# TensorE's order through an attention stage: a fixed order with a list of projections for each head, in place of a scheduler's

## The chip, the cores and the metric

The kernel runs on one core of a Trainium2 chip. The metric is the device time of one execution in microseconds. A core has a matrix engine (TensorE, in the profile PE, with its weight loads as PEld), a vector engine (VectorE, DVE), an activation engine (ScalarE, ACT), a general engine (GpSimd, POOL) and an engine that issues most of the transfers (SyncE, SP). Each works through a queue of its own in order, and they meet at semaphores.

## The reference

One layer of a streaming encoder over 512 frames of width 1024, all in float32:

```python
xn = rmsnorm(x, norm_mix_g)
q, k, v, xr, gr, ga, gb = split(xn @ w_in)
ya = chunked_band_attention(q, k, v, rel_table) @ w_attn_out    # 16 heads of 64
yb = (rg_lru(causal_depthwise_conv(xr)) * gelu(gr)) @ w_rnn_out
g_a, g_b = sigmoid([ga, gb] + b_merge)
h = x + (g_a * ya + g_b * yb) @ w_o
g, up = split(rmsnorm(h, norm_ffn_g) @ w_ffn_in)
out = rmsnorm(h + (silu(g) * up) @ w_ffn_out, final_norm_g)
```

In the attention each frame reads its own chunk of 64 frames and the eight before it, with a learned bias by relative distance for each head. With 512 frames the band reaches back to the start, so it is causal by chunks.

## The kernel before

Every float32 operand of a projection is split into a high and a low part (`split`, L78: ScalarE copies the high part, L80, VectorE subtracts it, L81), and a product is three matmuls, high-high, high-low and low-high (`mm3`, L72, lines L74 to L76). Weights are loaded to `raw` tiles and split to `whl` tiles; `weights` (L243) also prefetches the next chunk. Four `whl` buffers hold two chunks of weights, so a half of a new chunk is split when a projection has done with the half that had its buffer.

The order of the work is: normalize x, the projections and the recurrence of branch B, q and k of the first pair of heads, v of the first four heads, the output projection of branch B (`po_yb0` to `po_yb7`), then the attention, then `po_ya` (the output projection of the attention), `po_h`, and the feed-forward part.

The attention handles 16 heads, two to a pair. A pair needs a q tile and a k tile (`q_tile` L593, `k_tile` L604), four heads need four v tiles (`v_tile` L627). A q or k tile is 24 matmuls 512 wide, a v tile 24 matmuls 256 wide. Each is emptied from its bank by ScalarE and VectorE (q: L600 and L601; k: L611, L612, L613, and GpSimd's copy L614). For each head:

- `scores(h)` (L638): four score tiles s0 to s3, one for each block of 128 queries, 256, 256, 384 and 512 wide, two matmuls each (L651, L652). VectorE adds the bias and finds the negated maximum (L654, and a read of the accumulator m), ScalarE takes the exponential with the sum (L655), VectorE inverts the sums of all four (L656), GpSimd scales the four tiles (L658). The bias is a transfer (L424) and a memset of GpSimd (L425), with two buffers.
- `transposed(h, prob)` (L661): ten transposes (L670) of the probabilities to three banks, pT_0, pT_1 and pT_2, which are split to `pp` tiles for the next step.
- `weigh(h, pp)` (L679): eight matmuls (L690) to a bank `o`, emptied by ScalarE and VectorE (L691, L692).

The banks of the accumulator memory are eight: four with the tag "mm" (`mm_tile`, L69), two with "s", two with "t". Before the change the score tiles 0, 1 and 3 take the two "s" banks in turn and tile 2 an "mm" bank; pT_0 and pT_1 take "t"; pT_2, o and all projections of the attention take "mm".

The loop over the heads calls `transposed(h)`, `scores(h + 1)`, `fill`, `weigh(h)`, `fill`. `fill` takes projections from one list in the order q1, k1, q2, k2, v of heads 4 to 7, q3, and so on, ending with the gates `gate(0, 4)` to `gate(0, 7)` (tiles `po_ga`), until the work spent reaches a due sum. The calls do not fix the engines' order: the kernel is built under a scheduler that follows a simulated timeline and places every engine's instructions, TensorE's among them, by priority and by when it thinks they are ready. It chooses the bank of each tile as well. So in the program before, score tiles and weighings stand between matmuls of a projection; `s_3`, for instance, stands inside the projection that follows it.

Of the kernel before, what the change touches and what calls it, by code (L numbers as in the profile page):

```python
# [8 lines left out]
F32 = mybir.dt.float32  # L9
# [5 lines left out]
P = 128  # L15
D = 1024
S = 512
KT = D // P
NT = S // P
HEADS = 16  # L20
# [16 lines left out]
def block_kernel(ctx: ExitStack, tc: tile.TileContext, x, norm_mix_g, w_in, b_merge, rel_table,  # L37
# [25 lines left out]
    ps = ctx.enter_context(tc.tile_pool(name="ps", bufs=2, space=PSUM))  # L63
    dr = ctx.enter_context(tc.tile_pool(name="dr", bufs=1, space=bass.MemoryType.DRAM))

    def f(ap):
        return ap.bitcast(F32)

    def mm_tile(name, tag="mm"):  # L69
        return ps.tile([P, S], F32, tag=tag, bufs=4 if tag == "mm" else 2, name=name)  # L70
# [172 lines left out]
    def weights(name, ahead=1):  # L243
        prefetch(index[name] + 1 + ahead)
        return made[index[name]]

    def project(o, whl, c, xs, lo=0, hi=S):

        n = len(xs)
        for k in range(n):  # L250
            at = slice(c * P, (c + 1) * P)
            mm3(o[:, lo:hi], whl(0, k, at), whl(1, k, at),
                xs[k][:, 0, lo:hi], xs[k][:, 1, lo:hi], k == 0, k == n - 1)
# [108 lines left out]
    def features(pl, tag, name):  # L362

        t = pl.tile([P, KT, 2, S], F32R, tag=tag, name=name)
        return t, [t[:, k] for k in range(KT)]
# [13 lines left out]
    _, xnT = features(xnp, "xn", "xnT")  # L379
# [165 lines left out]
    def tile_of(name, c, tag="mm", ahead=1):  # L545

        whl = weights(name, ahead)
        if (name, c) in first:
            po = first[name, c]
            project(po, whl, c, xnT, 256, S)  # L550
        else:
            po = mm_tile(f"po_{name}_{c}", tag)
            project(po, whl, c, xnT)
        return po
# [5 lines left out]
    def gate(w, j):  # L560
        po = tile_of(f"g{'ab'[w]}{j - j % 2}", j % 2)
        act.activation((ta, zB)[w][j], po[:], AF.Tanh, bias=hb[:, 16 + 8 * w + j:17 + 8 * w + j], scale=0.5)
# [30 lines left out]
    def q_tile(pr):  # L593
        po = mm_tile(f"po_q{pr}")
        project(po, weights(f"qk{pr}"), 0, xnT)
        q = qk_pool(pr).tile([P, 2, S], F32R, tag="qk", bufs=3, name=f"q{pr}")
        for e in range(2):
            own, other = halves(e)
            src = backwards(po[own, :])
            act.activation(blocks(q[own, e]), src, AF.Copy, scale=0.125)  # L600
            dve.scalar_tensor_tensor(blocks(q[other, e]), src, 0.125, blocks(f(q[own, e])), ALU.mult, ALU.subtract)  # L601
        qk[pr] = [q]

    def k_tile(pr):  # L604
        po = mm_tile(f"po_k{pr}")
        project(po, weights(f"qk{pr}"), 1, xnT)
        kh = qk_pool(pr).tile([P, 2, S], F32R, tag="qk", bufs=3, name=f"kh{pr}")
        kl = qk_pool(pr).tile([P, 2, S], F32R, tag="qk", bufs=3, name=f"kl{pr}")
        for e in range(2):
            own, other = halves(e)  # L610
            act.activation(kh[own, e], po[own, :], AF.Copy)  # L611
            dve.tensor_sub(kl[own, e], po[own, :], f(kh[own, e]))  # L612
            act.activation(kh[other, e], po[own, :], AF.Copy)  # L613
            pool.tensor_copy(kl[other, e], kl[own, e])  # L614
        qk[pr] += [kh, kl]
# [11 lines left out]
    def v_tile(gr, t):  # L627
        wv = weights(f"v{gr}")
        po = mm_tile(f"po_v{gr}_{t}", "mm" if gr else "t")
        for k in range(KT):  # L630
            mm3(po[:, 0:256], xnT[k][:, 0, t * P:(t + 1) * P], xnT[k][:, 1, t * P:(t + 1) * P],
                wv(0, k, whole), wv(1, k, whole), k == 0, k == KT - 1)
        v = aw.tile([P, 2, 4, HD], F32R, tag="v", bufs=8, name=f"v{gr}_{t}")
        split(v[:, :, 0::3], v[:, :, 1:3], po[:, 0:256].rearrange("p (a b d) -> p a b d", a=2, b=2))
        vs.setdefault(gr, []).append(v)


    def scores(h):  # L638
        pr, e = divmod(h, 2)
        q, kh, kl = qk[pr]  # L640
        bias = bias_tile(h)
        lsum = cp.tile([P, NT], F32, tag="lsum", bufs=2, name=f"l{h}")
        nmax = cp.tile([P, NT], F32, tag="nmax", bufs=2, name=f"m{h}")
        rl = cp.tile([P, NT], F32, tag="rl", bufs=2, name=f"rl{h}")
        prob = [aw2.tile([P, (qb + 1) * P], F32, tag=f"p{qb}", name=f"p{h}_{qb}") for qb in range(NT)]
        for qb in range(NT):
            w = (qb + 1) * P
            wm = max(w, 256)
            sc = mm_tile(f"s{h}_{qb}") if qb == 2 else ps.tile([P, S], F32, tag="s", bufs=2, name=f"s{h}_{qb}")
            qs = q[:, e, qb * P:(qb + 1) * P]  # L650
            pe.matmul(sc[:, 0:wm], qs, kh[:, e, 0:wm], start=True, stop=False)  # L651
            pe.matmul(sc[:, 0:wm], qs, kl[:, e, 0:wm], start=False, stop=True)  # L652

            dve.tensor_tensor_reduce(prob[qb][:], sc[:, 0:w], bias[:, S - w:S], -1.0, 3e38, ALU.add, ALU.min, nmax[:, qb:qb + 1])  # L654
            act.activation(prob[qb][:], prob[qb][:], AF.Exp, bias=nmax[:, qb:qb + 1], scale=-1.0, accum_out=lsum[:, qb:qb + 1])  # L655
        dve.reciprocal(rl[:], lsum[:])  # L656
        for qb in range(NT):
            pool.tensor_scalar(prob[qb][:], prob[qb][:], rl[:, qb:qb + 1], 1.0, ALU.mult, ALU.mult)  # L658
        return prob

    def transposed(h, prob):  # L661

        pp = [aw2.tile([P, 2, S], F32R, tag="pt", bufs=4, name=f"pp{h}_{i}") for i in range(3)]
        pool.memset(f(pp[2][:, :, 256:384]), 0.0)
        for i, kbs in enumerate(((0,), (1,), (2, 3))):
            pt = mm_tile(f"pT{h}_{i}") if i == 2 else ps.tile([P, S], F32, tag="t", bufs=2, name=f"pT{h}_{i}")
            for kb in kbs:
                for qb in range(kb, NT):
                    at = qb - min(kb, 2) if kb < 3 else 2
                    pe.transpose(pt[:, at * P:(at + 1) * P], prob[qb][:, kb * P:(kb + 1) * P], ident[:])  # L670
            for at, lo, n in (((0, 0, 512),), ((0, 0, 384),), ((0, 0, 256), (384, 256, 128)))[i]:
                split(pp[i][:, 0, at:at + n], pp[i][:, 1, at:at + n], pt[:, lo:lo + n])
        return pp
# [5 lines left out]
    def weigh(h, pp):  # L679
        pr, e = divmod(h, 2)  # L680
        own, other = halves(e)
        if e == 0:
            oacc.append(tg_.tile([P, S], F32, tag="tg", name=f"oacc{pr}"))
        acc = oacc[pr]
        po = mm_tile(f"o{h}")
        for kb in range(NT):
            i, lo, n = ((0, 0, 512), (1, 0, 384), (2, 0, 256), (2, 256, 256))[kb]
            st = vs[pr // 2][kb][:, pr % 2, 2 * e:2 * e + 2].rearrange("p a d -> p (a d)")
            for part in range(2):
                pe.matmul(po[:, S - n:S], st, pp[i][:, part, lo:lo + n], start=kb == 0 and part == 0, stop=kb == NT - 1 and part == 1)  # L690
        act.activation(acc[own, :], po[other, :], AF.Copy)  # L691
        dve.tensor_add(acc[own, :], po[own, :], acc[own, :])  # L692
        if e == 1:
            if pr % 2 == 0:
                aT_pairs.append(rnp.tile([P, 2, 2, S], F32R, tag="big", bufs=4, name=f"aT{pr}"))
            o = aT_pairs[-1][:, pr % 2]
            split(blocks(o[:, 0]), blocks(o[:, 1]), backwards(acc[:]))
            aT.append(o)


    steps = []
    for pr in range(1, HEADS // 2):
        steps.append((1.0, lambda pr=pr: q_tile(pr)))
        steps.append((1.0, lambda pr=pr: k_tile(pr)))
        if pr in (2, 4, 6):
            for t in range(NT):
                steps.append((0.5, lambda pr=pr, t=t: v_tile(pr // 2, t)))
    for j in range(4, KT):
        steps.append((1.0, lambda j=j: gate(0, j)))
    spent = 0.0  # L710

    def fill(upto):
        nonlocal spent
        while steps and spent < upto:
            w, what = steps.pop(0)
            what()
            spent += w

    for t in range(NT):
        v_tile(0, t)  # L720
# [1 line left out]
    for j in range(KT):  # L722
        if j == 6:
            prob = scores(0)
        po = mm_tile(f"po_yb{j}")
        project(po, weights(f"yb{j - j % 2}"), j % 2, rnn)
        dve.scalar_tensor_tensor(zB[j], zB[j], 1.0, po[:], ALU.add, ALU.mult)
    for h in range(HEADS):
        pp = transposed(h, prob)
        if h + 1 < HEADS:  # L730
            prob = scores(h + 1)
        fill(1.25 + 1.5 * h)
        weigh(h, pp)
        fill(2.0 + 1.5 * h)
    aw2_stack.close()
    wo_stack, wop = opened("wo", 4)
    extra["wo1"] = wop
# [3 lines left out]
    _, mT = features(xnp, "xn", "mT")  # L741
# [113 lines left out]
    sc_stack, sc = opened("sc", 2)  # L855
# [83 lines left out]
    ks = list(range(0, FT, 4))  # L939
# [51 lines left out]
```

## Time and profile before

| | |
|---|---|
| median of 3 runs | 888.18 us (887.58 to 888.22) |
| the profiled execution | 887.22 us |
| its span, first to last instruction | 885.4 us |
| TensorE's clock | 1.000 of full |
| TensorE busy, share of the span | 98% |
| the attention, from the first transposes to the last weighing | about 248 to 449 us of the span |

The span is the time between the first and the last instruction of the profiled execution; 1.8 us of its own time lie around it. A row of the timeline has the start from the span's start in us, the duration in us, the engine, the line of the code, the operation, what it writes and reads with the shapes, and how many instructions are merged in the row. In brackets stands how long the engine had been idle ahead of it, and which instruction ended that. A row of the windows has the stretch, its length, then the busy time of PE, PEld, DVE, ACT and POOL, TensorE's granted clock, and the transfers' share and rate. The steps from the start of one matmul to that of the next are shorter than the durations, since matmuls overlap.

### The profile page before, as it was taken

Reading aid. Unit: us, or ns where it says so; the run is one execution under the profiler, and the core shown is the slowest. Engines: PE = TensorE matmul, PEld = TensorE weight load, DVE = VectorE, ACT = ScalarE, POOL = GpSimd, SP = SyncE. Lnnn points to the kernel's source line nnn. Section 1 sums busy time; section 2 is a strip of 40 time slices with the busy share of each in tenths; the row PEclk is TensorE's granted clock in tenths of the full one; section 3 lists DMA queues with packets and bytes.
Section 4 is the critical chain, followed back from the end, with each engine's and each line's share of the span. In section 5 each row is a group of like instructions: output and inputs, shape, how many; then the busy total and the mean of one; then the engine's idle time right before and its main releaser. Section 6 shows DMA issues by size and latency. Waiting matters only on the chain.

```text
span 885.4 us, 13311 instructions
## 1 busy us (share of the span) xinstructions
PE 871.9 (98%) x5220; PEld 776.5 (88%) x5220; DVE 548.4 (62%) x872; ACT 472.7 (53%) x839; POOL 112.1 (13%) x157
## 2 busy tenths in 40 slices
PE   7999999999999999999999999999999999999997
PEld 5988888888888889898888889999999999888886
DVE  5776556563456675665447556888878887553203
ACT  7566646652256676676533466656555555723203
POOL 4013112220022222322100000000000001300100
PEclk9999999999999999999999999999999999999999
DMA  7223233433333233232223720524333332353002
GB/s 266 89 79 106 85 95 95 121 95 95 97 95 95 72 91 89 72 97 83 59 79 126 261 72 25 163 77 126 113 95 95 101 127 84 121 180 124 28 1 96
DMA packets 86080, 90.11 MB, mean 102 GB/s; under 512 B 5376, under 2 KB 74608, under 8 KB 86016
## 3 DMA queue, kind: packets, MB, share of 16 engines
q1 hardware_dynamic: 84640, 85.78, 31.5%
q10 hardware_dynamic: 1376, 3.47, 1.0%
q8 instruction: 41, 0.67, 0.3%
q14 instruction: 23, 0.19, 0.1%
HBM read 87.10 MB, written 2.14 MB: 101 GB/s over the span
## 4 chain that ended last, share of the span: by engine, by line
PE 96%; DVE 1%; SPq 1%; DMA 1%; ACT 1%; issue 1%; POOL 0%; ACTq 0%
PE po_out L74 5%; PE po_out L75 5%; PE po_out L76 5%; PE p_fg L74 2%; PE o L690 2%; PE p_fg L76 2%; PE p_fu L76 2%; PE p_fu L75 2%; PE p_fg L75 2%; PE p_fu L74 2%; PE pT L670 2%; PE po_v L75 2%; PE po_v L76 2%; PE po_v L74 2%; PE po_q L74 2%; PE po_q L75 2%
## 5 line engine op out<-in xcount | busy, mean ns | idle before, releaser
L75 PE MATMUL po_out<-whl_fo,act_hi 128*128 128x512 f32 (+1 forms) x198 | 72.5, 366 | 0.0
L74 PE MATMUL po_out<-whl_fo,act_hi 128*128 128x512 f32 (+1 forms) x198 | 72.3, 366 | 0.0
L76 PE MATMUL po_out<-whl_fo,act_lo 128*128 128x512 f32 (+1 forms) x198 | 71.7, 365 | 0.0
L81 DVE TENSOR_TENSOR whl_fo<-raw_fo,whl_fo 128x1024 fp32r<-128x1024 f32 x22 | 27.8, 1273 | 44.3 <-ACT whl_fo L80 43.9
L658 POOL TENSOR_SCALAR p<-p,rl 128x128 f32<-128x128 f32 (+1 forms) x64 | 36.1, 587 | 142.0 <-DVE rl L656 142.0
L875 POOL TENSOR_TENSOR act_lo<-act,act_hi 128x1024 fp32r<-128x1024 f32 x4 | 10.9, 2719 | 322.9 <-ACT act_hi L874 320.8
L80 ACT ACTIVATE whl_fo<-raw_fo 128x1024 fp32r<-128x1024 f32 x22 | 23.0, 1059 | 48.9 <-PE po_out L76 33.9
L654 DVE CUSTOM_DVE_ANT_0 p<-s,bias 128x384 f32<-128x384 f32 (+2 forms) x64 | 29.6, 485 | 21.5 <-PE s L652 20.9
L76 PEld LDWEIGHTS po_out<-whl_fo,act_lo 128*128 128x128 f32 x198 | 37.3, 189 | 6.0
L74 PEld LDWEIGHTS po_out<-whl_fo,act_hi 128*128 128x128 f32 x198 | 37.4, 189 | 6.0
L75 PEld LDWEIGHTS po_out<-whl_fo,act_hi 128*128 128x128 f32 x198 | 37.4, 189 | 5.9
L655 ACT ACTIVATE p<-p,m 128x384 f32<-128x384 f32 (+2 forms) x64 | 35.7, 561 | 12.6 <-DVE m L654 12.2
L76 PE MATMUL po_v<-whl_v,xnT 128*128 128x256 f32 x128 | 36.2, 283 | 0.0
L75 PE MATMUL po_v<-whl_v,xnT 128*128 128x256 f32 x128 | 36.2, 282 | 0.0
L74 PE MATMUL po_v<-whl_v,xnT 128*128 128x256 f32 x128 | 36.1, 282 | 0.0
L81 DVE TENSOR_TENSOR pp<-pT,pp 128x512 fp32r<-128x512 f32 (+1 forms) x64 | 29.3, 485 | 5.3 <-ACT pp L80 5.0
L75 PE MATMUL po_xr<-xnT,whl_xr 128*128 128x512 f32 (+1 forms) x80 | 27.9, 354 | 0.6 <-DVE xnT L358 0.6
L81 DVE TENSOR_TENSOR whl_fg_s<-s_fg,whl_fg_s 128x1024 fp32r<-128x1024 f32 x20 | 25.6, 1295 | 3.7 <-ACT whl_fg_s L80 3.7
L74 PE MATMUL po_gr<-xnT,whl_gr 128*128 128x512 f32 (+1 forms) x80 | 27.8, 349 | 0.1
L76 PE MATMUL po_gr<-xnT,whl_gr 128*128 128x512 f32 (+1 forms) x80 | 27.5, 348 | 0.3 <-DVE whl_gr L81 0.3
L75 PE MATMUL po_gr<-xnT,whl_gr 128*128 128x512 f32 (+1 forms) x80 | 27.6, 347 | 0.0
L74 PE MATMUL po_xr<-xnT,whl_xr 128*128 128x512 f32 (+1 forms) x80 | 26.6, 351 | 0.8 <-ACT xnT L357 0.8
(348 smaller groups left out, 3044.9 us busy)
## 6 DMA issues: line engine op xcount, KB each, us to landing
raw_fg<-in_w_ffn_in_dram SPq DMA_DIRECT2D x24, 512.0 KB, 4.5
raw_fu<-in_w_ffn_in_dram SPq DMA_DIRECT2D x22, 512.0 KB, 3.8
raw_fo<-in_w_ffn_out_dram SPq DMA_DIRECT2D x22, 512.0 KB, 4.2
raw_qk<-in_w_in_dram SPq DMA_DIRECT2D x32, 256.0 KB, 3.1
raw_xr<-in_w_in_dram SPq DMA_DIRECT2D x8, 512.0 KB, 4.6
raw_gr<-in_w_in_dram SPq DMA_DIRECT2D x8, 512.0 KB, 3.4
raw_ga<-in_w_in_dram SPq DMA_DIRECT2D x8, 512.0 KB, 3.9
raw_gb<-in_w_in_dram SPq DMA_DIRECT2D x8, 512.0 KB, 3.6
```

The costliest lines, as they stand in the source:

```text
L74: pe.matmul(o, sh, mh, start=start, stop=False, skip_group_check=parts)
L75: pe.matmul(o, sh, ml, start=False, stop=False, skip_group_check=parts)
L76: pe.matmul(o, sl, mh, start=False, stop=stop, skip_group_check=parts)
L80: act.activation(hi, src, AF.Copy)
L81: dve.tensor_sub(lo, src, f(hi))
L654: dve.tensor_tensor_reduce(prob[qb][:], sc[:, 0:w], bias[:, S - w:S], -1.0, 3e38, ALU.add, ALU.min, nmax[:, qb:qb + 1])
L655: act.activation(prob[qb][:], prob[qb][:], AF.Exp, bias=nmax[:, qb:qb + 1], scale=-1.0, accum_out=lsum[:, qb:qb + 1])
L658: pool.tensor_scalar(prob[qb][:], prob[qb][:], rl[:, qb:qb + 1], 1.0, ALU.mult, ALU.mult)
L670: pe.transpose(pt[:, at * P:(at + 1) * P], prob[qb][:, kb * P:(kb + 1) * P], ident[:])
L690: pe.matmul(po[:, S - n:S], st, pp[i][:, part, lo:lo + n], start=kb == 0 and part == 0, stop=kb == NT - 1 and part == 1)
L875: (pool if i in (0, 1, 2, 4) else dve).tensor_sub(lo[:], o[:], f(hi[:]))
```

## The change

Three things. The loop over the heads stands in a block in which TensorE's instructions keep the order of the calls (`tc.manual_schedule`); the other engines and the banks are still left to the scheduler. The list with due sums is replaced by `laid(h)`, which gives each head the projections ahead of its weighing and those behind it. And score tile 3 takes an "mm" bank, as tile 2 does.

```diff
-            sc = mm_tile(f"s{h}_{qb}") if qb == 2 else ps.tile([P, S], F32, tag="s", bufs=2, name=f"s{h}_{qb}")
+            sc = mm_tile(f"s{h}_{qb}") if qb >= 2 else ps.tile([P, S], F32, tag="s", bufs=2, name=f"s{h}_{qb}")
...
-    steps = []
-    for pr in range(1, HEADS // 2):
-        steps.append((1.0, lambda pr=pr: q_tile(pr)))
-        steps.append((1.0, lambda pr=pr: k_tile(pr)))
-        if pr in (2, 4, 6):
-            for t in range(NT):
-                steps.append((0.5, lambda pr=pr, t=t: v_tile(pr // 2, t)))
-    for j in range(4, KT):
-        steps.append((1.0, lambda j=j: gate(0, j)))
-    spent = 0.0
-
-    def fill(upto):
-        nonlocal spent
-        while steps and spent < upto:
-            w, what = steps.pop(0)
-            what()
-            spent += w
+    def laid(h):
+        m, at = divmod(h, 4)
+        qs, ks, va = (lambda pr: lambda: q_tile(pr)), (lambda pr: lambda: k_tile(pr)), (lambda t: lambda: v_tile(m + 1, t))
+        if h >= 12:
+            return [lambda: gate(0, h - 8)], []
+        first_, second = 2 * m + 2, 2 * m + 3
+        return {0: (([qs(1), ks(1)] if m == 0 else []) + ([] if m == 0 else [qs(first_)]), [qs(first_)] if m == 0 else []),
+                1: ([ks(first_)], [va(0)]),
+                2: ([va(1), va(2)], [va(3)]),
+                3: ([qs(second)], [ks(second)])}[at]
...
-    for h in range(HEADS):
-        pp = transposed(h, prob)
-        if h + 1 < HEADS:
-            prob = scores(h + 1)
-        fill(1.25 + 1.5 * h)
-        weigh(h, pp)
-        fill(2.0 + 1.5 * h)
+    with tc.manual_schedule(engines={mybir.EngineType.PE}):
+        for h in range(HEADS):
+            pp = transposed(h, prob)
+            if h + 1 < HEADS:
+                prob = scores(h + 1)
+            before, after = laid(h)
+            for what in before:
+                what()
+            weigh(h, pp)
+            for what in after:
+                what()
```

So head 0 has q1, k1, its weighing, q2; head 1 has k2, weighing, one v tile; head 2 two v tiles, weighing, one v tile; head 3 q3, weighing, k3; head 4 q4 and the weighing; heads 5 to 7 as 1 to 3; head 8 as head 4, and so on; heads 12 to 15 one gate each and the weighing. Around the loop, score tile 3 of head 0 also moves: it stands ahead of `po_yb6`, not inside it.

## The prediction

> **What bounds the kernel now.** I read the page first (busy time, chain), then TensorE's waits, then the timeline of TensorE in the attention, and last the order in which the built programs place their instructions on each engine.
>
> ```profile
> PE 871.9 (98%) x5220; PEld 776.5 (88%) x5220; DVE 548.4 (62%) x872; ACT 472.7 (53%) x839; POOL 112.1 (13%) x157
> PE 96%; DVE 1%; SPq 1%; DMA 1%; ACT 1%; issue 1%; POOL 0%; ACTq 0%
> ```
>
> TensorE is 98% busy and holds 96% of the chain that ends last. The change adds and removes no matmul, so it can win only TensorE's lost time in the attention, and every wait it adds there is paid in full. The waits by TensorE between 255 and 455 us are one line:
>
> ```profile
> PE s L651 <- ACT kh L613: 2.0, 4, 0.5
> ```
>
> That is too low: a matmul is shown longer than the step to the next one, so a short wait hides in "busy". I count steps instead (TensorE's timeline; start, duration, engine, line):
>
> ```profile
> 262.17 1.25 PE L670 MATMUL pT<-ident,p 128*128 128x128 f32 x10
> 263.92 0.68 PE L651 MATMUL s<-kh,q 128*128 128x256 f32 x3 [0.50 <-ACT kh L613]
> 264.84 0.46 PE L74 MATMUL po_q<-xnT,whl_qk 128*128 128x512 f32 x1
> ...
> 274.87 0.39 PE L74 MATMUL po_k<-xnT,whl_qk 128*128 128x512 f32 x1
> 277.36 0.39 PE L76 MATMUL po_k<-xnT,whl_qk 128*128 128x512 f32 x1
> 278.93 0.28 PE L651 MATMUL s<-kh,q 128*128 128x256 f32 x1
> 279.16 0.34 PE L651 MATMUL s<-kh,q 128*128 128x384 f32 x1
> 279.63 0.28 PE L75 MATMUL po_v<-whl_v,xnT 128*128 128x256 f32 x1
> 281.54 0.28 PE L76 MATMUL po_v<-whl_v,xnT 128*128 128x256 f32 x1
> ...
> 302.61 1.25 PE L670 MATMUL pT<-ident,p 128*128 128x128 f32 x10
> 303.62 0.42 PE L651 MATMUL s<-kh,q 128*128 128x384 f32 x1
> 304.52 0.39 PE L74 MATMUL po_k<-xnT,whl_qk 128*128 128x512 f32 x1
> 309.99 1.44 PE L690 MATMUL o<-pp,v 128*128 128x512 f32 x8
> 311.26 1.25 PE L670 MATMUL pT<-ident,p 128*128 128x128 f32 x10
> ...
> 411.15 0.68 PE L651 MATMUL s<-kh,q 128*128 128x256 f32 x3 [0.50 <-ACT kh L613]
> ```
>
> From these: 11 steps of a q or k tile take 277.36 - 274.87 = 2.49, so 24 take 5.43. 16 steps of a v tile take 1.91, so 24 take 2.87. Ten transposes and the two wide score tiles take 304.52 - 302.61 = 1.91, the two narrow ones 2 x (279.16 - 278.93) = 0.46: **transposes and scores together 2.37**. A weighing takes 311.26 - 309.99 = 1.27.
>
> **The change part by part.** *What goes.* The order repeats every four heads: four times transposes, scores and weighing, two q, two k and four v tiles: 4 x 3.64 + 4 x 5.43 + 4 x 2.87 = 47.76. The first and the fourth wait for kh stand 411.15 - 263.92 = 147.23 apart, 49.08 for each four heads. So 1.32 are lost per period, 3.95 in three. The first kh wait lies ahead of that: 263.92 - 262.17 = 1.75 where 303.62 - 302.61 = 1.01 is the step without a wait, 0.74. Head 15's transposes wait twice for GpSimd's scaled probabilities:
>
> ```profile
> 433.42 2.06 POOL L658 TENSOR_SCALAR p<-p,rl 128x128 f32<-128x128 f32 x4 [11.06 <-DVE rl L656]
> 434.30 0.20 PEld L670 LDWEIGHTS pT<-ident,p 128*128 128x128 f32 x2 [0.32 <-POOL p L658]
> 434.86 0.31 PEld L670 LDWEIGHTS pT<-ident,p 128*128 128x128 f32 x3 [0.36 <-POOL p L658]
> ```
>
> That is 0.68. Together 3.95 + 0.74 + 0.68 = **5.4 lost**, and it is all that can be won. The kh waits do go: the lists put each k tile a head or more ahead of its scores (k1 is followed by a weighing and q2, 1.27 + 5.43, ahead of scores(2)).
>
> *What comes.* The tag "mm" has four banks. After a head that has a q, k or v tile behind its weighing, TensorE comes to the next head with that tile's bank still being emptied; the transposes of blocks 2 and 3 take a bank, the score tiles 2 and now also 3 take two. All four are full, and the next projection, 2.37 after the first transpose, waits for whichever bank the builder gave it. In the built program po_k2 (head 1) has the bank of s2_2, and po_q4, po_q6 and po_ga4 (heads 4, 8, 12) that of score tile 2 of the same head; each waits for VectorE's read of it at L654. VectorE's program order up to that read:
>
> ```
> head 1:  q2 (L601) | pp1_0 | p2_0 | pp1_1 | p2_1 | pp1_2 | p2_2 -> po_k2
> head 4:  kl3 (L612) | p5_0 | p5_1 | whl_v2_4 (1024 wide) | p5_2 -> po_q4
> ```
>
> Heads 8 and 12 stand as head 4 does, with whl_v3_4 and whl_ga6_4. In head 4 the scalar engine's order is kh3, whl_v2_4, then pp4. The steps of before that price these (VectorE and ScalarE in the timeline):
>
> ```profile
> 302.81 0.59 ACT L600 ACTIVATE q<-po_q 64x512 fp32r<-64x512 f32 x1 [2.76 <-PE po_q L76]
> 303.43 0.68 DVE L601 SCALAR_TENSOR_TENSOR q<-po_q,q 64x512 fp32r<-64x512 f32 x1 [2.66 <-ACT q L600]
> 304.15 0.69 DVE L81 TENSOR_TENSOR pp<-pT,pp 128x512 fp32r<-128x512 f32 x1
> 304.76 0.55 DVE L654 CUSTOM_DVE_ANT_0 p<-s,bias 128x384 f32<-128x384 f32 x1
> 305.23 0.08 DVE L654 DVE_READ_ACCUMULATOR2_ANT m<- 128x1 f32 x1
> 305.23 0.88 DVE L81 TENSOR_TENSOR pp<-pT,pp 128x384 fp32r<-128x384 f32 x2
> 306.03 0.68 DVE L654 CUSTOM_DVE_ANT_0 p<-s,bias 128x512 f32<-128x512 f32 x1
> ...
> 310.68 1.05 ACT L80 ACTIVATE whl_v<-raw_v 128x1024 fp32r<-128x1024 f32 x1
> 310.81 0.68 DVE L612 TENSOR_TENSOR kl<-po_k,kh 64x512 fp32r<-64x512 f32 x1 [0.95 <-ACT kh L611]
> 311.76 1.49 DVE L81 TENSOR_TENSOR whl_v<-raw_v,whl_v 128x1024 fp32r<-128x1024 f32 x1 [0.26 <-ACT whl_v L80]
> 313.17 0.67 DVE L692 TENSOR_TENSOR oacc<-o,oacc 64x512 f32<-64x512 f32 x1
> 315.21 0.28 DVE L654 CUSTOM_DVE_ANT_0 p<-s,bias 128x128 f32<-128x128 f32 x1
> 315.42 0.42 DVE L654 CUSTOM_DVE_ANT_0 p<-s,bias 128x256 f32<-128x256 f32 x1
> 315.76 0.55 DVE L81 TENSOR_TENSOR pp<-pT,pp 128x384 fp32r<-128x384 f32 x1
> ```
>
> Head 1, from the first transpose, when q2's matmuls have just been issued: VectorE's q starts at 0.82 (303.43 - 302.61), pp1_0 at 1.54, p2_0 at 2.15; p2_0 takes 0.21 (315.21 to 315.42), p2_1 0.34 (to 315.76), pp1_1 and pp1_2 together 0.80 (305.23 to 306.03), p2_2 0.47 and the read of its minimum 0.08: 2.15 + 0.21 + 0.34 + 0.80 + 0.55 = 4.05. VectorE started 0.03 after ScalarE's end here (302.81 + 0.59, 303.43); I allow TensorE 0.05. Against 2.37: **a wait of 1.7**.
>
> Head 4: kl3 starts 0.82 after k3's last matmul (310.81 - 309.99) and ends at 1.50; the first scores are read from about 1.6 (an estimate: their second matmul starts a step or two after 1.01, and matmuls show 0.28 to 0.42). p5_0 and p5_1 to 2.15. whl_v2_4 waits for ScalarE's half, which ends at 310.68 + 1.05 - 309.99 = 1.74, so it starts at 2.15; its step was 1.41 in the row at 311.76, where GpSimd worked beside it, shown as 1.49, so 0.08 less than shown; I take 1.15 from a row of 1.24 that has only GpSimd's scaling beside it, as there is little of GpSimd's work here:
>
> ```profile
> 308.62 1.24 DVE L81 TENSOR_TENSOR whl_v<-raw_v,whl_v 128x1024 fp32r<-128x1024 f32 x1 [0.76 <-ACT whl_v L80]
> ```
>
> That gives 3.30, and with p5_2 3.85, TensorE at 3.9 to 4.15: waits of 1.5 to 1.8, **1.6 each in three heads**, 4.8. A restart costs some 0.07 (the first projection matmul after a wait shows 0.46 at 264.84, the others 0.39), 0.3 for four. In head 14 the bank of o(13) is emptied behind whl_ya0_4 on both engines, which I put at 0.2 by the same steps. The k tiles of heads 5 and 9 wait for q's second half, ready at 2.2 against 2.37: nothing, but with 0.15 to spare. All else has cover: v tiles are emptied 0.6 or more ahead of need, and head 15's probabilities now start behind a score tile issued 5.4 earlier, so its 0.68 goes.
>
> Bounds of the four waits: were VectorE to read tile 2 at once, the tile would be ready at 2.2 and read by 2.75, 0.4 each, 1.7 in all; with VectorE's large step at 1.41 and 0.3 of queue besides, 2.2 each, 8.8. I take the middle of what the queue gives, since the order is fixed in the program and its steps were measured.
>
> **The sum:** 1.7 + 4.8 + 0.3 + 0.2 = 7.0 come and 5.4 go, net **+1.6 to +1.7**. The profiled execution took 887.22 (span 885.4 and 1.8 around it): 888.9. The median of runs is 0.96 above it: 888.18 + 1.7 = **889.9**. From yb7 to the end of the attention alone do matmuls change place; from po_ya2 on all engines keep their order, and no slack stands there to give time back.
>
> [...] Before, TensorE stopped four times at kh, and the windows of 49 us around them show the full clock:
>
> ```profile
> 262.00:311.00 49.00, 48.50 (x297) 43.34 (x296) 32.56 (x77) 33.13 (x77) 13.42 (x27) 1.00 0.31 87
> 884.00:885.00 1.00, 0.00 (x0) 0.00 (x0) 0.00 (x0) 0.00 (x0) 0.00 (x0) 0.79 0.00 0
> ```
>
> The clock fell only at the end, in the window 884 to 885, about five us after the last matmul (issued near 879). [...]
>
> **Rivals.**
> *Bank in time* (faster). If VectorE reads the third score tile ahead of the other work, the four waits fall to 1.7 in all: 1.7 + 0.5 - 5.4 = -3.2, 885.0. The change is faster once the four waits sum to less than 4.9, 1.2 each. For it: the weights' split has no need to stand ahead of p5_2. Against: it stands there in the program. Chance 0.08; halfway, -1 or about 887, another 0.12.
> *Transposes wait too* (much slower). p(6) and p(10) are scaled behind a bias memset, whose load is issued only after p's last read; the scaling of four took 2.06 above, but 3.04 beside a large VectorE step:
>
> ```profile
> 307.95 3.04 POOL L658 TENSOR_SCALAR p<-p,rl 128x128 f32<-128x128 f32 x4 [10.19 <-DVE rl L656]
> DMA to landing us min/median/max: 3.2/3.3/4.6
> ```
>
> By the steps above p6_3 is read at about 5.2 of head 5, so its load lands at 8.6 and the scaling ends by 11: in time for the transposes at 12. With 4.6 and 3.04 it is 13, some 0.8 late in two heads; with the bank waits at 2.2 each and k4, k6 late as well, the total is about +5.5, 893.7. Chance 0.22.
> [...] Chance 0.02.
>
> My forecast has 0.56, its own range 888.9 to 891.5.
>
> **How the numbers follow.** 0.2% is 1.8 us, about what a measurement of this kernel can tell from no change, and my sum lies on that line. What I may have missed adds waits, none of it removes any, so I give the forecast 0.34 above the line and 0.22 within it. Slower: 0.34 + 0.22 + 0.02 = 0.58. Same: 0.22 + 0.12 = 0.34. Faster: 0.08. The range takes in the halfway case and most of the slow one: 887.0 to 893.7.
>
> **What would show it.** In the changed profile TensorE's waits should no longer name kh, and should name po_k2, po_q4, po_q6 and po_ga4 waiting for VectorE's m at L654, 1.5 to 1.7 each as the gap behind the scores; head 15's transposes should not wait. No such waits, or waits on p from GpSimd of a like size, would prove the account wrong; so would a clock under 1.00 in the attention.

## The result, and the profile after

The changed kernel takes 890.6 us (889.64 to 891.58, 7 runs) where the kernel before takes 887.58 (887.27 to 888.32, 7 runs beside it): a ratio of 1.0032, with an interval of 1.0023 to 1.0041. It is slower by 3.0 us. The forecast was a net of 1.7 and a time of 889.9, in a range from 887.0 to 893.7. The profiled execution took 889.64, its span is 887.8: 2.4 over the span before. The executions of each of the two differ by 1 to 2 us, and about 1 us of that can arise ahead of the attention: the same first transposes start at 247.55 in this trace and at 248.48 in the trace of the first experiment below, where TensorE's granted clock was 0.98 in the first 100 us and not 1.00.

First the page of the kernel after: busy time, and the engines' shares of the chain that ended last.

```profile
PE 871.4 (98%) x5220; PEld 776.1 (87%) x5220; DVE 551.8 (62%) x872; ACT 473.1 (53%) x839; POOL 111.0 (13%) x157
PE 95%; DVE 2%; SPq 1%; DMA 1%; issue 1%; ACT 1%; DVEq 0%; ACTq 0%
```

TensorE does the same 5220 matmuls and still carries the chain; VectorE's part of the chain went from 1% to 2%. Next TensorE's waits in the kernel after, between 250 and 455 us (who waits for whom: us in total, times, longest us):

```profile
PE po_q L74 <- DVE m L654: 2.8, 2, 1.4
PE po_k L74 <- DVE m L654: 1.6, 1, 1.6
PE po_ga L74 <- DVE m L654: 1.4, 1, 1.4
```

Before, the only line was kh. It is gone, and four waits for VectorE's read of a score tile stand in its place. The idle times shown are short again, since a matmul is shown longer than its step (0.39 for a step of 0.23 at 269.51). The timeline of TensorE gives them whole:

```profile
269.51 0.39 PE L651 MATMUL s<-kh,q 128*128 128x512 f32 x1
269.74 0.40 PE L652 MATMUL s<-kl,q 128*128 128x512 f32 x1
271.69 0.51 PE L74 MATMUL po_k<-xnT,whl_qk 128*128 128x512 f32 x1 [1.56 <-DVE m L654]
272.03 0.40 PE L75 MATMUL po_k<-xnT,whl_qk 128*128 128x512 f32 x1
...
310.49 0.40 PE L652 MATMUL s<-kl,q 128*128 128x512 f32 x1
312.28 0.50 PE L74 MATMUL po_q<-xnT,whl_qk 128*128 128x512 f32 x1 [1.39 <-DVE m L654]
...
361.99 0.51 PE L74 MATMUL po_q<-xnT,whl_qk 128*128 128x512 f32 x1 [1.39 <-DVE m L654]
...
411.72 0.50 PE L74 MATMUL po_ga<-xnT,whl_ga 128*128 128x512 f32 x1 [1.39 <-DVE m L654]
...
429.84 0.40 PE L652 MATMUL s<-kl,q 128*128 128x512 f32 x1
430.29 0.50 PE L74 MATMUL po_ga<-xnT,whl_ga 128*128 128x512 f32 x1
430.63 0.40 PE L75 MATMUL po_ga<-xnT,whl_ga 128*128 128x512 f32 x1
...
437.14 1.25 PE L670 MATMUL pT<-ident,p 128*128 128x128 f32 x10
438.15 0.48 PE L74 MATMUL po_ga<-xnT,whl_ga 128*128 128x512 f32 x1
```

A 512 wide step without a wait is 269.74 - 269.51 = 0.23. Head 1's wait is then 271.69 - 269.74 - 0.23 = 1.72, head 4's 312.28 - 310.49 - 0.23 = 1.56. Heads 8 and 12 show the same idle time of 1.39, so 1.56 each. Head 14's is 430.29 - 429.84 - 0.23 = 0.22. After each the next step is 0.33 to 0.34 (272.03 - 271.69 in head 1) where 0.23 is usual, about 0.11 more. Head 15's ten transposes take 438.15 - 437.14 = 1.01: no wait. **What came: 1.72 + 3 x 1.56 + 0.22 + 5 x 0.11 = 7.2.** VectorE's timeline in head 4 shows the queue that sets it:

```profile
309.96 0.29 DVE L654 CUSTOM_DVE_ANT_0 p<-s,bias 128x128 f32<-128x128 f32 x1
...
310.18 0.42 DVE L654 CUSTOM_DVE_ANT_0 p<-s,bias 128x256 f32<-128x256 f32 x1
...
310.52 1.22 DVE L81 TENSOR_TENSOR whl_v<-raw_v,whl_v 128x1024 fp32r<-128x1024 f32 x1
311.66 0.55 DVE L654 CUSTOM_DVE_ANT_0 p<-s,bias 128x384 f32<-128x384 f32 x1
312.14 0.08 DVE L654 DVE_READ_ACCUMULATOR2_ANT m<- 128x1 f32 x1
```

Two narrow reads, the 1024 wide subtraction of the weights, then the read of score tile 2, done near 312.2; q4 starts at 312.28. In head 1 nothing 1024 wide is in the queue: there a half of q2 and the probabilities of the head (`pp`) stand ahead, the read ends at 271.63, and k2 starts at 271.69. The granted clock stayed at 1.00 with head 1's wait in the stretch (windows of the kernel after):

```profile
262.00:311.00 49.00, 47.33 (x291) 42.08 (x289) 31.73 (x69) 31.18 (x68) 10.80 (x24) 1.00 0.31 90
```

### The profile page after: what moved, and what is told of

Read it like the earlier page. It is cut to its first block, busy times and chain, and to the rows that moved or that the text cites. A ratio compares the mean times of both kernels' runs of the same rounds, so it can differ in the third digit from the quotient of the medians.

```text
span 887.8 us, 13325 instructions
## 1 busy us (share of the span) xinstructions
PE 871.4 (98%) x5220; PEld 776.1 (87%) x5220; DVE 551.8 (62%) x872; ACT 473.1 (53%) x839; POOL 111.0 (13%) x157
## 4 chain that ended last, share of the span: by engine, by line
PE 95%; DVE 2%; SPq 1%; DMA 1%; issue 1%; ACT 1%; DVEq 0%; ACTq 0%
PE po_out L74 5%; PE po_out L76 5%; PE po_out L75 5%; PE p_fg L74 2%; PE o L690 2%; PE p_fg L76 2%; PE p_fu L76 2%; PE p_fg L75 2%; PE p_fu L75 2%; PE p_fu L74 2%; PE po_v L75 2%; PE po_v L76 2%; PE po_ga L74 2%; PE po_v L74 2%; PE pT L670 2%; PE po_q L74 2%
## 5 line engine op out<-in xcount | busy, mean ns | idle before, releaser
L655 ACT ACTIVATE p<-p,m 128x128 f32<-128x128 f32 (+1 forms) x64 | 35.8, 561 | 11.0 <-DVE m L654 10.7
L654 DVE CUSTOM_DVE_ANT_0 p<-s,bias 128x128 f32<-128x128 f32 (+1 forms) x64 | 29.9, 485 | 1.1 <-issue 0.6
L81 DVE TENSOR_TENSOR whl_qk<-raw_qk,whl_qk 128x1024 fp32r<-128x1024 f32 x16 | 20.5, 1282 | 14.0 <-ACT whl_qk L80 14.0
L75 PE MATMUL po_xr<-xnT,whl_xr 128*128 128x512 f32 (+1 forms) x80 | 27.9, 354 | 0.6 <-DVE xnT L358 0.6
L74 PE MATMUL po_q<-xnT,whl_qk 128*128 128x512 f32 x64 | 25.2, 394 | 2.8 <-DVE m L654 2.8
L74 PE MATMUL po_gr<-xnT,whl_gr 128*128 128x512 f32 (+1 forms) x80 | 27.8, 349 | 0.1
L76 PE MATMUL po_gr<-xnT,whl_gr 128*128 128x512 f32 (+1 forms) x80 | 27.5, 348 | 0.3 <-DVE whl_gr L81 0.3
```

The costliest lines, as they stand in the source:

```text
L74: pe.matmul(o, sh, mh, start=start, stop=False, skip_group_check=parts)
L75: pe.matmul(o, sh, ml, start=False, stop=False, skip_group_check=parts)
L76: pe.matmul(o, sl, mh, start=False, stop=stop, skip_group_check=parts)
L81: dve.tensor_sub(lo, src, f(hi))
```

## The experiments

The first theory was the prediction's: the time is lost where a projection waits for a bank that VectorE has not read. The rivals: TensorE's fixed order as such, the bank as such, VectorE's load as such, a softmax that is late whatever the bank. Each ratio below is to the kernel before on the same chip, where it had medians of 887.3 to 887.9.

**Another bank for the four projections** (a change to the kernel after, as all are that name no other):

```diff
-        po = mm_tile(f"po_q{pr}")
+        po = mm_tile(f"po_q{pr}", "s" if pr in (4, 6) else "mm")
...
-        po = mm_tile(f"po_k{pr}")
+        po = mm_tile(f"po_k{pr}", "s" if pr == 2 else "mm")
...
-        po = tile_of(f"g{'ab'[w]}{j - j % 2}", j % 2)
+        po = tile_of(f"g{'ab'[w]}{j - j % 2}", j % 2, "s" if (w, j) == (0, 4) else "mm")
```

> The changed kernel with one thing different: the four projections that waited (k2 in head 1, q4, q6 and ga4 in heads 4, 8, 12) take their bank from the two of the score tiles 0 and 1 instead of the four that score tiles 2 and 3, transposes and projections share. TensorE's order is untouched. Theory (the loss is the queue on VectorE ahead of its read of score tile 2): in the two banks they wait only for the read of score tile 0, done 2.0 to 2.5 us after the first transpose where TensorE comes at 2.39, so each wait falls to 0 to 0.1. The waits of 1.73 and 3 x 1.56 and their four restarts of 0.11 go: 6.8 less than the changed kernel, 883.8, and about 4 less than the kernel before. Rival (the softmax is late whatever the bank): TensorE comes 1.6 earlier to the next transposes, which then wait for GpSimd's scaled probabilities, and the time falls by 0 to 3 only. Rival (the rearranged order itself costs): no more than 1 less.

Measured: 886.02, ratio 0.998 (0.9971 to 0.9989). With TensorE's tiles in the same order in both traces, 0.5% went, some 4.6 us, and the kernel is faster than before: the bank waits were what made the change a loss. The forecast was 6.8. The rest went to waits that came up behind the ones removed; this kernel's TensorE waits between 250 and 455, and its largest in the timeline:

```profile
PE s L651 <- DVE q L601: 1.3, 2, 0.8
PE pT L670 <- POOL p L658: 0.2, 1, 0.2
```

```profile
318.21 0.28 PE L652 MATMUL s<-kl,q 128*128 128x256 f32 x1
319.26 0.36 PE L651 MATMUL s<-kh,q 128*128 128x256 f32 x1 [0.78 <-DVE q L601]
```

q4 and q6 now sit in the bank that score tile 1 of heads 6 and 10 wants, and VectorE empties their second half late: 319.26 - 318.21 - 0.12 = 0.93 in this head.

**Score tile 3 swapped with tile 1 in these two heads** (a change to the kernel just shown):

```diff
-            sc = mm_tile(f"s{h}_{qb}") if qb >= 2 else ps.tile([P, S], F32, tag="s", bufs=2, name=f"s{h}_{qb}")
+            sc = mm_tile(f"s{h}_{qb}", "mm" if qb in ((1, 2) if h in (6, 10) else (2, 3)) else "s")
```

> The kernel with the four projections in the score tiles' two banks (1.45 us below the kernel before), with one thing different: in heads 6 and 10 score tile 1 takes a bank of the four and score tile 3 one of the two. There score tile 1 waited 0.94 and 0.68 for VectorE's second half of q4 and q6 in its bank (rows at 319.26 and 368.52, restarts of 0.08 behind them). Theory: score tile 3 comes 0.8 later than score tile 1, so 0.1 to 0.2 is left of each wait: 1.3 to 1.6 less, 884.4 to 884.7, 2.7 to 3.1 below the kernel before. Rival (the softmax of those heads becomes the limit, since VectorE stands behind q either way): score tiles 2 and 3 are read no earlier, and the transposes of heads 6 and 10 wait for probabilities: less than 0.5 gained.

Measured: 885.23, ratio 0.9971 (0.996 to 0.9982). The gain over the kernel above is 0.8, smaller than the 1.3 to 1.6 forecast, in the right direction; the interval of each reaches the other's median, so the gain is not clear of noise. One wait for q is left in TensorE's list of waits, of 0.2 as shown, where the theory left 0.1 to 0.2 in each head.

**The weights' subtraction to GpSimd in heads 4, 8 and 12:**

```diff
-                if len(made) == 0 and k:
+                if (len(made) == 0 and k) or (k and name in ("v2", "v3", "ga6")):
                     act.activation(hl[:, 0], raw[:], AF.Copy)
                     pool.tensor_sub(hl[:, 1], raw[:], f(hl[:, 0]))
```

> The changed kernel with one thing different: the low half of the 1024 wide weights tile of v2, v3 and ga6 is subtracted on GpSimd instead of VectorE, so that nothing 1024 wide stands on VectorE between the reads of score tiles 1 and 2 in heads 4, 8 and 12. Banks and TensorE's order are untouched. Theory: VectorE's read of score tile 2 in these three heads ends some 1.15 earlier, the three waits fall from 1.56 to about 0.4, head 1's 1.73 stays: 3 x 1.15 = 3.5 less than the changed kernel, about 887. Rival (GpSimd becomes late): its subtraction stands ahead of its scaling of the probabilities, and transposes wait for p in heads 5, 9 and 13, 1 to 2 each: no gain or slower, 889 to 893. Rival (another wait is behind the VectorE read): less than 1 gained.

Measured: 888.07, ratio 1.0002 (0.9993 to 1.0011): 2.5 less than the kernel after. TensorE's waits, and its timeline in head 4:

```profile
PE po_k L74 <- DVE m L654: 1.6, 1, 1.6
PE pT L670 <- POOL p L658: 0.6, 2, 0.3
PE po_q L74 <- DVE m L654: 0.5, 2, 0.3
PE po_ga L74 <- DVE m L654: 0.3, 1, 0.3
```

```profile
310.68 0.40 PE L652 MATMUL s<-kl,q 128*128 128x512 f32 x1
311.33 0.50 PE L74 MATMUL po_q<-xnT,whl_qk 128*128 128x512 f32 x1 [0.25 <-DVE m L654]
```

The wait fell to 311.33 - 310.68 - 0.23 = 0.42, the 0.4 of the theory, and head 1's stayed. The rival was right in part as well: the transposes of heads 5, 9 and 13 now wait for GpSimd and take 1.25, 1.76 and 1.47 where 1.01 is usual. That is 0.2 to 0.8 more each where the rival had 1 to 2, and 2.5 of the 3.5 is left.

**The same subtraction twice on VectorE:**

```diff
                     split(hl[:, 0], hl[:, 1], raw[:])
+                    if k and name in ("v2", "v3", "ga6"):
+                        dve.tensor_sub(hl[:, 1], raw[:], f(hl[:, 0]))
```

> The changed kernel with the 1024 wide subtraction of the second weights tiles of v2, v3 and ga6 done twice on VectorE (the same values written again). In the built order the second one stands behind the read of score tile 2, not ahead of it. Theory (the place in VectorE's queue costs, not VectorE's load): 3 x 1.2 more work on VectorE and no change of the time beyond 0.5: 890.1 to 891.1. Rival (VectorE is too busy in these heads, any work on it costs): 3 x 1.15 = 3.5 more, 894. In between: the second half of q or k is emptied later and one of the tight waits (k4, k6, head 14) opens: 0.5 to 1.5.

Measured: 891.27, ratio 1.0037 (1.0024 to 1.005), 0.4 to 0.7 more than the kernel after for three more steps of 1.22 us on VectorE: 0.2 above the range of the theory, far from the rival's 894, and within the noise of the kernel after (the interval takes in 1.0032). The second subtraction stands at 314.34, behind the read of tile 2, and the bank waits did not change (1.39 idle again at q4). So the bank waits come from the place in VectorE's queue and not from its load. The load is not quite free: in this trace the transposes of heads 5, 9 and 13 take 1.44, 1.29 and 1.31 where 1.01 is usual, 1.0 together, because they wait for p.

**q2 ahead of k2, not behind head 0's weighing:**

```diff
-        return {0: (([qs(1), ks(1)] if m == 0 else []) + ([] if m == 0 else [qs(first_)]), [qs(first_)] if m == 0 else []),
-                1: ([ks(first_)], [va(0)]),
+        return {0: (([qs(1), ks(1)] if m == 0 else []) + ([] if m == 0 else [qs(first_)]), []),
+                1: (([qs(first_)] if m == 0 else []) + [ks(first_)], [va(0)]),
```

> The changed kernel with one thing different: q2 moves from behind head 0's weighing to the place ahead of k2 in head 1, so that no projection is being emptied when head 1's transposes and scores take their banks. Theory: q2 then needs a bank that k1 left free, and k2 comes 5.43 later, long after VectorE's read of its bank: head 1's wait of 1.73 and its restart of 0.11 go, and the three of heads 4, 8 and 12 stay at 1.5 to 1.6: 1.8 less than the changed kernel, 888.6 to 888.8, still 1.1 to 1.3 above the kernel before. Rival (a wait comes back elsewhere): head 1's weighing comes a tile later and head 2's scores wait for k1 or q1 no longer, but head 2's transposes or head 3's scores wait for k2: gain under 0.5.

Measured: 890.6, ratio 1.0035 (1.0021 to 1.0048): nothing won, my theory missed. TensorE's timeline of this kernel:

```profile
262.31 1.25 PE L670 MATMUL pT<-ident,p 128*128 128x128 f32 x10
264.06 0.38 PE L651 MATMUL s<-kh,q 128*128 128x256 f32 x1 [0.49 <-ACT kh L613]
...
265.28 0.40 PE L652 MATMUL s<-kl,q 128*128 128x512 f32 x1
266.57 0.50 PE L74 MATMUL po_q<-xnT,whl_qk 128*128 128x512 f32 x1 [0.90 <-ACT kh L613]
```

The wait at k2 is gone, but q2 had covered the emptying of k1. Without it the scores wait 0.7 for kh, as in the kernel before (264.06 - 262.31 = 1.75 against 1.01), and q2 waits for k1's bank, 1.06 (266.57 - 265.28 - 0.23). I had called that bank free early; ScalarE's last copy from it stands behind its work on pp and ends near 266.5. The rival had the outcome (a gain under 0.5), with the waits in other heads than these.

**The parts of the change, one at a time.** Program order and lists, with score tile 3 in its old bank:

```diff
-            sc = mm_tile(f"s{h}_{qb}") if qb >= 2 else ps.tile([P, S], F32, tag="s", bufs=2, name=f"s{h}_{qb}")
+            sc = mm_tile(f"s{h}_{qb}") if qb == 2 else ps.tile([P, S], F32, tag="s", bufs=2, name=f"s{h}_{qb}")
```

> TensorE in program order and the lists as in the changed kernel, but score tile 3 stays in one of the two banks of the score tiles, as before the change. Theory: score tile 3 then waits behind VectorE's read of score tile 0 of the same head, by the program's order 0.6 to 1.1 in heads 0, 1, 5, 9 and 14, 0.5 in head 13 and next to nothing in the others, some 5.5 with restarts of 0.1 for seven; the waits of the projections go. Beside the changed kernel 0.5 to 1.5 less, 889 to 890, and still above the kernel before. Rival (the order alone is at fault, the bank brings something): it is slower than the changed kernel by over 1. Rival (the bank alone is at fault): it falls below the kernel before, 885 to 886.

Measured: 892.05, ratio 1.0045 (1.0032 to 1.0057). I had forecast less than the kernel after; by the ratios it is 1.2 more, and the two intervals overlap. Its waits, and the largest:

```profile
PE s L651 <- DVE m L654: 5.7, 10, 1.1
```

```profile
320.00 0.34 PE L652 MATMUL s<-kl,q 128*128 128x384 f32 x1
321.48 0.50 PE L651 MATMUL s<-kh,q 128*128 128x512 f32 x1 [1.14 <-DVE m L654]
```

All its waits are of the kind forecast, score tile 3 for VectorE's read of tile 0, but ten are shown where I had counted six or seven of note, and this one is 321.48 - 320.00 - 0.18 = 1.3 where I had 1.1. Under the program's order the new bank thus seems to bring about 1 us, not clear of noise.

The bank alone, in the kernel before (its list, and the scheduler ordering TensorE; the same line as the change has it):

> The kernel before, its scheduler's order and its steps, with score tile 3 in a bank of the four: the other half of the change alone. Theory: the waits for kh stay, since the order of k tiles and scores stays nearly as it was, and projections that come after four score tiles have a bank less; the scheduler places instructions by its own estimate of when a bank is free, so the price is between 0 and 4 over the kernel before. Rival (the bank is what costs, whatever the order): 3 or more over the kernel before, with the same waits behind VectorE's m as in the changed kernel. Rival (the order is what costs): within 0.5 of the kernel before, or below it.

Measured: 898.12, ratio 1.0114 (1.01 to 1.0127), about 10 more where I had 0 to 4. The rival's time (3 or more) holds here, its mechanism only in small part. TensorE's waits between 250 and 455, and its timeline in head 1:

```profile
PE s L651 <- ACT kh L613: 5.3, 7, 1.1
PE po_q L74 <- ACT kh L613: 2.7, 3, 0.9
PE po_k L74 <- DVE m L654: 2.1, 3, 0.7
PE po_ga L74 <- ACT kh L613: 0.9, 1, 0.9
```

```profile
265.71 0.46 PE L651 MATMUL s<-kh,q 128*128 128x512 f32 x1
267.31 0.50 PE L74 MATMUL po_q<-xnT,whl_qk 128*128 128x512 f32 x1 [0.91 <-ACT kh L613]
```

The kh waits multiply (they were 2.0 in four), and projections now wait for banks, four of them for one that a k tile still holds; only three of the fourteen waits are for VectorE's m. The expectation took TensorE's order to stay nearly as it was. It did not: with the new bank the scheduler put score tile 3 ahead of q2 (265.71, then 267.31), where before it stood at 270.17, behind 23 of q2's matmuls. So the 10 us are the price of the bank together with the order that the scheduler then chose, and the run does not part the two.

Lists and bank, with the scheduler ordering TensorE:

```diff
-    with tc.manual_schedule(engines={mybir.EngineType.PE}):
+    with ExitStack():
```

> The changed kernel with one thing different: the builder's scheduler, and not the program, orders TensorE through the attention (lists and banks as changed). It draws score tiles 0 and 1 of the next head but one ahead of projections, so that those stand behind k tiles still being emptied. Theory (the program's order is what takes the kh waits away): the waits for kh come back in heads 6, 8, 10, 12 and 14, 0.5 to 1.2 each, and bank waits stay: 1 to 6 above the changed kernel, 891.5 to 896.5. Rival (TensorE in program order is what costs, since it cannot step over a full bank): at or below the kernel before, 885.5 to 888.

Measured: 888.08, ratio 1.001 (1.0001 to 1.0019): by the ratios 2.0 below the kernel after, where I had 1 to 6 above. Both halves of my reason were wrong. No wait for kh is left, so the lists remove them without the program's order; and the bank wait of head 4 is smaller:

```profile
310.29 0.39 PE L652 MATMUL s<-kl,q 128*128 128x512 f32 x1
310.87 0.50 PE L74 MATMUL po_q<-xnT,whl_qk 128*128 128x512 f32 x1 [0.19 <-DVE m L654]
```

That is 310.87 - 310.29 - 0.23 = 0.35 for 1.56. In this kernel only score tiles 2 and 3 stand behind head 4's transposes: the scheduler had placed tiles 0 and 1 earlier, so VectorE had read them, and it reads tile 2 ahead of the 1024 wide subtraction.

The lists alone (the kernel above with the old bank line, `qb == 2`):

> The list of projections for each head alone: the builder's scheduler orders TensorE, and score tile 3 stays in one of the two banks, both as before the change. Theory (from the run with lists and bank under the scheduler, which had no wait for kh left): it is the lists that take away the kh waits of 0.84 and the waits of score tile 3; the bank adds nothing without the program's order. So it stands at or below the run with both, 886 to 888, within 1 of the kernel before. Rival (lists need the bank): score tile 3 holds back the narrow score tiles of the next head, which wait for VectorE's read of tile 1: 889 to 892.

Measured: 885.36, ratio 0.9979 (0.997 to 0.9987): faster than the kernel before, by the lists and the order that the scheduler makes of them. It is 0.6 below the 886 to 888 that I had; no gain over the kernel before was forecast beyond 1 us, and it is about 2. One wait is left, in head 2. Its rows in TensorE's timeline, then GpSimd's:

```profile
274.48 0.39 PE L651 MATMUL s<-kh,q 128*128 128x512 f32 x1
...
280.48 0.40 PE L652 MATMUL s<-kl,q 128*128 128x512 f32 x1
282.24 1.56 PE L670 MATMUL pT<-ident,p 128*128 128x128 f32 x6 [1.36 <-POOL p L658]
```

```profile
281.32 0.15 POOL L425 MEMSET bias<- 64x64 f32 x1 [3.46 <-DMA bias<-ext_d]
281.56 2.30 POOL L658 TENSOR_SCALAR p<-p,rl 128x128 f32<-128x128 f32 x4
```

This is the prediction's second rival, in another kernel: probabilities behind a memset that waits for a bias load. Here score tile 3 is late, because it stands behind k2 (274.48). So the lists were changed once more, in head 1:

```diff
-                1: ([ks(first_)], [va(0)]),
+                1: (([va(0)], [ks(first_)]) if m == 0 else ([ks(first_)], [va(0)])),
```

> The kernel with the lists alone (885.36, 0.9979 of the kernel before) with one thing different: in head 1 the tile v1_0 comes ahead of the weighing and k2 behind it. With the lists alone one wait is left, 2.27 with its restarts: head 2's transposes wait for GpSimd's scaled probabilities, because score tile 3 of head 2 stands behind k2 (row at 274.48), its read by VectorE lets go of a bias tile whose next load lands only at 281.3, and GpSimd's scaling stands behind that. Theory: score tile 3 then stands behind v1_0, 0.6 shorter in TensorE and free of the wait for the bank, some 3 earlier, and the scaling ends about when the transposes come: 1.3 to 2.2 less, 883.2 to 884.1. Rival (the bias load is late whatever score tile 3 does, or k2 is now late for the scores): within 0.5 of the lists alone.

Measured: 882.97, ratio 0.9956 (0.9942 to 0.9971), 4.3 below the kernel before and the fastest of all, 0.2 below the range forecast. Windows of this kernel and of the kernel after over the whole attention:

```profile
247.00:455.00 208.00, 208.00 (x1207) 184.21 (x1206) 133.73 (x298) 133.29 (x296) 49.71 (x102) 1.00 0.29 86
```

```profile
247.00:455.00 208.00, 202.21 (x1177) 178.24 (x1176) 128.93 (x291) 131.12 (x292) 49.15 (x101) 1.00 0.29 83
```

TensorE is busy for 208.00 of 208.00 us; in the kernel after, 5.8 were idle as shown. GpSimd's scaling of head 2 starts at 275.95 here and needs no bias load first.

The parts together, ratios to the kernel before:

| TensorE's order | list | score tile 3 in "s" | score tile 3 in "mm" |
|---|---|---|---|
| scheduler | old, due sums | 1 | 1.0114 |
| scheduler | for each head | 0.9979 | 1.0010 |
| program | for each head | 1.0045 | 1.0032 (the change) |

Under the scheduler the lists win 0.2% with the old bank and 1.0% with the new one. With the same lists and bank, the program's order takes 0.2% (new bank) to 0.7% (old bank). Under the program's order, where TensorE's tiles stand in the same order in both runs, the new bank seems to win a little (the intervals overlap), since there score tile 3 would wait itself. Under the scheduler the run with the new bank is 0.3% to 1.1% slower, but the scheduler also orders TensorE otherwise in those runs, so this is not the price of the bank alone. The old list in program order was not tried.

## Why the prediction was right

Its sign and its mechanism held: the four waits came where, for what and as long as it said. The net was forecast too small, 1.7 where the medians differ by 3.0 and the profiled executions by 2.4. That the time lies only 0.7 above 889.9 is in part luck: the forecast stood on a median of 888.18 for the kernel before, and beside the changed kernel it ran at 887.58.

- *The kh waits and head 15's wait go:* right, no such wait is left. The reason given, the lists, is shown by the two runs with lists under the scheduler, which have no kh wait either.
- *Four bank waits, 1.7 + 4.8:* measured 1.72 + 4.68. The queues of VectorE read from the program, with durations from before, gave each wait within 0.05, and not by errors that cancel: from head 4's first transpose at 308.34 the large subtraction starts after 2.18 (forecast 2.15) and the read of tile 2 starts after 3.32 (forecast 3.30); in head 1 the read ends 4.04 after the first transpose at 267.59 (forecast 4.05). The choice of 1.15 for the 1024 wide step was right: 311.66 - 310.52 = 1.14. The two runs that move or double this subtraction show that it sets the three.
- *Restarts 0.3, head 14 0.2:* measured 0.55 for five stops and 0.22. The 0.07 was read at 264.84, a matmul that does not stand right behind a wait; behind one it is 0.11.
- *5.4 removed:* this is the term that was mis-sized. 7.2 came and the span grew by 2.4, so about 4.8 went. The prediction took 49.08 less a sum of steps, 47.76, as lost in each four heads. In the kernel after, q4 starts at 312.28 and q6 at 361.99; 49.71 less q6's wait of 1.56 and q4's restart of 0.11 is 48.04 for the same work. The fastest kernel above, which has no wait of TensorE left, needs as much from q5 to q7, 391.45 - 343.38 = 48.07:

```profile
343.38 0.40 PE L74 MATMUL po_q<-xnT,whl_qk 128*128 128x512 f32 x1
...
391.45 0.40 PE L74 MATMUL po_q<-xnT,whl_qk 128*128 128x512 f32 x1
```

So about 0.28 of each 1.32 was not lost time and could not be won. Three times that is 0.84, a little over the 0.6 that are missing (5.4 against 4.8). The prediction's own rows hold part of it: k3 runs from 304.52 to the weighing at 309.99, 5.47, where 24 times the mean of eleven later steps gave 5.43; in two q and two k tiles that is 0.16. That the fastest kernel, with every wait gone, stands 4.3 below the kernel before and not 5.4 fits.

- *Transposes wait too:* not in the kernel after. It is the next limit all the same: it came up at 0.2 to 0.3 idle in the runs where TensorE came earlier or where GpSimd or VectorE had more to do, and at 1.4 with the lists alone.
- *Bank in time:* worked out at 3.2 below before; the run that gave the four projections another bank reached 1.5 below, since the next waits came up. The run that took the subtraction from VectorE shows the rival's own case in three heads: 0.42 is left of each wait, where it had 0.4.
- *The 0.02 in the chance of slower, and a clock under 1.00:* no run shows a clock that falls at the bank waits. The kernel after has 1.00 from 262 to 311, with head 1's wait of 1.72 in it, and the kernel with the bank alone, with fourteen waits shown, has 1.00 over the whole attention:

```profile
247.00:455.00 208.00, 197.03 (x1140) 171.15 (x1139) 127.67 (x288) 129.94 (x290) 45.76 (x101) 1.00 0.28 80
```

## What to carry to other kernels

A change of several parts can hide a gain inside a loss: here the list of projections alone wins, and the fixed order that came with it takes more than that back. Before fixing an engine's order by hand, look at what each consumer of its banks has queued ahead of the read; a bank is free when that queue says so, not when the tile is written (in head 4 of the kernel after, score tile 2 has its second matmul issued at 310.08 and its read done near 312.2). And when a wait is taken away, name the one that stands right behind it: two of the runs here (another bank, GpSimd's subtraction) won less than forecast for that reason, and one (q2 ahead of k2) won nothing.

## What the runs showed of the hardware

- After each bank wait TensorE's first projection matmul takes a step of 0.33 to 0.34 where 0.23 is usual (271.69 to 272.03, 312.28 to 312.61): about 0.11 for each stop, besides the wait. A wait is not the only thing that lengthens it: behind head 15's transposes, which did not wait, the first step is 0.31 (438.15 to 438.46).
- The 1024 wide subtraction takes VectorE a step of 1.14 (310.52 to 311.66 in the kernel after), and GpSimd 2.40 as shown. In the kernel that moved it, GpSimd's next scaling of p starts at 316.57, behind a memset that waited for a bias load, and not at 315.73 as in the kernel after (GpSimd's timeline of the kernel that moved it):

```profile
310.86 2.40 POOL L237 TENSOR_TENSOR whl_v<-raw_v,whl_v 128x1024 fp32r<-128x1024 f32 x1
...
316.33 0.15 POOL L425 MEMSET bias<- 64x64 f32 x1 [1.58 <-DMA bias<-ext_d]
316.57 2.07 POOL L658 TENSOR_SCALAR p<-p,rl 128x128 f32<-128x128 f32 x4
```
